# Wide products in a split-precision transformer kernel: one of 512 columns for two of 256

## The chip, the cores and the metric

The kernel runs on one core of a Trainium2 chip, in one launch. The metric is the device time of an execution in microseconds (us); the kernel before takes a median of 1346.6 us in three runs (1344.37 to 1347.13). A core has a matrix engine (PE, with its weight loads PEld), a vector engine (DVE), an activation engine (ACT), a general engine (POOL) and a queue engine (SP) that here issues nearly all DMAs. PE writes only into PSUM, which has 8 banks of 512 float32 columns; the other engines read the results from there.

## What is computed

The input has 256 tokens of width 1024. A first layer (adaLN modulation, grouped-query attention beside spatial gating, an output projection, then an expert-choice layer of 16 experts whose weights are streamed from HBM), a second layer of latent attention, and a third, "forgetting" layer are applied in turn. The two places that the change touches are these.

```
mix_l = jnp.concatenate([gqa_attend(ql, k_all, v_all),
                         spatial_gating(hl, w_gm, v_gain, w_s, b_s)], axis=-1)
xl_new = xl + gt1 * (mix_l @ w_out)              # first output projection, 256x1024 @ 1024x1024
xl_new = xl_new + gt2 * expert_choice_ffn(modulate(xl_new, g_ffn, sh2, sc2), ...)
```

The forgetting layer projects its normalised input to queries, keys, values, forget logits and gates (16 heads of 64). A running sum of the log forget gates along the tokens is added, as a difference between query and key positions, to the scores ahead of a causal softmax; the attended values are multiplied by a gate (a sigmoid, computed through tanh) and projected by `o_w_out`; a final norm follows.

## The kernel before

Every float32 operand of a large product is kept as two parts, hi (rounded by a cast on ACT) and lo (the rest, a subtraction on DVE or POOL), and a product is three: hi.hi, hi.lo and lo.hi, added up in PSUM (`mm3`, L142). With 256 tokens as columns each of the three is a product of 128x128 weights with 256 columns. `cols8(w, k, ...)` picks chunk k of 8 along the contracted width, from both parts.

The program is straight-line, and the order of the code is the order on each engine: nothing is rescheduled. PSUM tiles are given out by `bank`, which takes the first of a list of free banks, and `free` puts a bank back at the list's end; a matmul group that takes a bank waits until the engine that read it last is through. SBUF has 23 slots of 1 MB with the same kind of list, filled by DMAs on the SP queue when a slot comes free. `split` issues hi and lo of a weight tile. `later` collects DVE steps that `flush` puts out at fixed points.

First output projection (L948 on): 8 output tiles of 128 rows by 256 tokens, each 8 chunks of `mm3` and one DVE step that scales the product and adds it to the residual `xT`; squares for the norm and the router's logits follow tile by tile, and after the last the routing, the gather and the experts' first products `p_h`.

The forgetting layer: queries and keys are computed in tiles of 256 features (`q_tile`, `k_tile`: one bank for the two 128-feature chunks, transposed, features on partitions), evicted by `qk_scaled` (one DVE step for each chunk: product times scale times the row of reciprocal norms `rb2`). Values come in tiles of 256 features, tokens on partitions, evicted by ACT (`v_tile`). Gates come in 8 chunks (`gate`): a DVE step, tanh on ACT, a DVE step. The running sum of the log forget gates (`fx`) is a chain of small DVE and ACT steps, transposed as `p_ct`. Attention goes in 8 pairs of heads through a software pipeline: step i computes scores and softmax numerators of pair i (`soft_a`: `p_s` on PE, bias and row extremes on DVE, exponentials on ACT), transposes pair i-1 (`soft_b`), normalises pair i on DVE (`soft_n`) and multiplies pair i-2 with the values (`soft_c`, `p_o`). The table `fills` names the projections that go into each step in between, and `FSP` the splits of weights. For the first pair, q0, k0, v0, the norm row (`p_bc`), q1 and k1 go ahead.

## Time and profile before

| | |
|---|---|
| median of three runs | 1346.6 us |
| the profiled execution | 1347.84 us |
| its span in the profile | 1346.1 us |
| first output projection, in the trace | until 169.0 us |
| experts, mostly weight DMA | about 182 to 1060 us |
| forgetting layer's values, queries, keys, gates | 1214 to 1314 us |
| output projection and final norm | 1314 to 1346 us |

Times in the trace count from the span's start. Rows of a timeline give the start, the time the instruction took (its end may overlap the next one's start), the engine, the line, the operation, out<-in and the shapes. The rows used are shown in a section of their own, ahead of the prediction.

### The profile page before, as it was taken

Reading aid. Unit: us, or ns where it says so; the run is one execution under the profiler, and the core shown is the slowest. Engines: PE = TensorE matmul, PEld = TensorE weight load, DVE = VectorE, ACT = ScalarE, POOL = GpSimd, SP = SyncE. Lnnn points to the kernel's source line nnn. Section 1 sums busy time; section 2 is a strip of 40 time slices with the busy share of each in tenths; the row PEclk is TensorE's granted clock in tenths of the full one; section 3 lists DMA queues with packets and bytes.
Section 4 is the critical chain, followed back from the end, with each engine's and each line's share of the span. In section 5 each row is a group of like instructions: output and inputs, shape, how many; then the busy total and the mean of one; then the engine's idle time right before and its main releaser. Section 6 shows DMA issues by size and latency. Waiting matters only on the chain.

```text
span 1346.1 us, 16926 instructions
## 1 busy us (share of the span) xinstructions
PE 1072.6 (80%) x6795; PEld 516.1 (38%) x6795; DVE 436.1 (32%) x1172; ACT 266.5 (20%) x538; POOL 128.9 (10%) x181
## 2 busy tenths in 40 slices
PE   6999987777677687777767777776766799999998
PEld 3875942111112111111211111121111287899996
DVE  2756552111012011111201111120212168837974
ACT  2536410000000000000000000000000156653563
POOL 1000100000000000000000000000000113781530
PEclk9999999878978787887979888798888799999999
DMA  9997699999999999999999999999999993274230
GB/s 374 398 395 296 237 383 427 427 426 427 427 427 427 427 427 427 427 427 427 427 426 428 426 427 426 427 426 427 427 428 425 384 349 119 68 269 153 95 126 32
DMA packets 112638, 482.76 MB, mean 359 GB/s; under 512 B 8010, under 2 KB 57424, under 8 KB 61104
## 3 DMA queue, kind: packets, MB, share of 16 engines
q1 hardware_dynamic: 111456, 479.10, 87.0%
q0 software_dynamic: 848, 2.48, 0.6%
q8 instruction: 54, 0.88, 0.2%
q14 instruction: 24, 0.20, 0.0%
q10 hardware_dynamic: 256, 0.10, 0.0%
HBM read 480.59 MB, written 1.06 MB: 358 GB/s over the span
## 4 chain that ended last, share of the span: by engine, by line
DMA 63%; PE 29%; DVE 4%; POOL 2%; ACT 1%; issue 1%; ACTq 0%; SPq 0%; DVEq 0%; POOLq 0%
DMA w<-in_w_dram 63%; PE p_aT L136 5%; PE p_aN L136 3%; PE p_gate L136 3%; POOL lo L166 2%; PE p_out L136 2%; PE p_s L136 2%; PE p_oo L136 2%; PE p_y L136 1%; PE p_o L136 1%; PE p_h L136 1%; PE p_mod L136 1%; PE p_aF L136 1%; PE p_lat L136 1%; PE p_pt L1415 1%
## 5 line engine op out<-in xcount | busy, mean ns | idle before, releaser
L136 PE MATMUL p_y<-w,hidT 128*32 128x512 f32 (+1 forms) x1088 | 240.4, 631 | 65.7 <-DMA w<-in_w_dram 58.8
L136 PE MATMUL p_h<-w,rows_k 128*32 128x512 f32 x1024 | 169.2, 753 | 91.2 <-DMA w<-in_w_dram 91.1
L136 PE MATMUL p_h<-w,rows_q 128*32 128x512 f32 x1024 | 170.5, 759 | 82.4 <-DMA w<-in_w_dram 81.3
L166 POOL TENSOR_TENSOR lo<-w,hi 128x256 fp32r<-128x256 f32 (+1 forms) x136 | 102.4, 789 | 973.4 <-ACT hi L162 957.1
L136 PEld LDWEIGHTS p_y<-w,hidT 128*32 128x32 f32 x1088 | 56.0, 116 | 251.9 <-issue 144.5
L1152 DVE SCALAR_TENSOR_TENSOR ysl<-p_y,ig,ysh 128x512 fp32r<-128x512 f32 (+1 forms) x34 | 24.4, 719 | 267.5 <-ACT ysh L1151 266.0
L136 PEld LDWEIGHTS p_h<-w,rows_k 128*32 128x32 f32 x1024 | 24.2, 119 | 214.5 <-DMA w<-in_w_dram 189.4
L136 PEld LDWEIGHTS p_h<-w,rows_q 128*32 128x32 f32 x1024 | 24.9, 119 | 200.0 <-DMA w<-in_w_dram 171.0
L1151 ACT ACTIVATE ysh<-p_y,ig 128x512 fp32r<-128x512 f32 (+1 forms) x34 | 22.4, 662 | 398.2 <-PE p_y L136 398.2
L1053 DVE TENSOR_SCALAR oh<-p_ix,cst,rs 128x32 f32<-128x32 f32 x30 | 7.9, 306 | 267.5 <-PE p_ix L136 267.5
L1075 ACT COPY xr<-p_g 128x256 f32<-128x256 f32 x16 | 6.0, 372 | 420.2 <-PE p_g L136 420.2
L162 ACT CAST hi<-w 128x2048 fp32r<-128x2048 f32 (+3 forms) x41 | 71.3, 1759 | 26.4 <-DMA w<-in_e_w_in_dram 19.1
L166 DVE TENSOR_TENSOR lo<-w,hi 128x2048 fp32r<-128x2048 f32 (+2 forms) x24 | 48.2, 2026 | 24.0 <-ACT hi L162 22.8
L1156 DVE SCALAR_TENSOR_TENSOR xT<-p_sc,m,xT 128x256 f32<-128x256 f32 x128 | 51.8, 475 | 4.0 <-PE p_sc L136 4.0
L1138 DVE TENSOR_TENSOR hid<-s,p_h 128x512 f32<-128x512 f32 x16 | 11.0, 688 | 83.9 <-PE p_h L136 83.9
L136 PE MATMUL p_aT<-y2h,hi 128*128 128x256 f32 x128 | 36.8, 287 | 0.6 <-ACT y2h L1227 0.6
L136 PE MATMUL p_aT<-y2l,hi 128*128 128x256 f32 x128 | 36.3, 284 | 0.1
L136 PE MATMUL p_aT<-y2h,lo 128*128 128x256 f32 x128 | 36.2, 283 | 0.0
L1076 DVE COPY xr<-p_g 128x256 f32<-128x256 f32 x16 | 6.8, 425 | 84.1 <-ACT xr L1075 84.1
L1393 ACT ACTIVATE pr<-pr,st 128x128 f32<-128x128 f32 x64 | 28.5, 447 | 25.8 <-DVE st L1389 25.8
L1408 DVE TENSOR_SCALAR pr<-pr,st 128x128 f32<-128x128 f32 x64 | 30.9, 545 | 0.6
L136 PE MATMUL p_mod<-w,cm 128*32 128x512 f32 x192 | 26.7, 642 | 0.8 <-ACT cm L466 0.8
(491 smaller groups left out, 1709.7 us busy)
## 6 DMA issues: line engine op xcount, KB each, us to landing
w<-in_w_dram SPq DMA_DIRECT2D x376, 1024.0 KB, 19.6
w<-in_w_mod_dram SPq DMA_DIRECT2D x24, 1024.0 KB, 10.1
w<-in_o_w_in_dram SPq DMA_DIRECT2D x16, 1024.0 KB, 8.2
w<-in_w_dram SPq DMA_DIRECT2D x16, 512.0 KB, 8.0
w<-in_w_in_dram SPq DMA_DIRECT2D x7, 1024.0 KB, 17.3
...
```

The costliest lines, as they stand in the source:

```text
L136: PE.matmul(o, lhsT, rhs, start=start, stop=stop, skip_group_check=True)
L162: S.copy(r_(hi[:, c_]), t[:, c_])
L166: eng.tensor_tensor(r_(lo[:, d_]), t[:, d_], hi[:, d_], op=OP.subtract)
L1053: V.tensor_scalar(oh[b], p[:, 0:n], table(C_TCOL + b, 1), rs2[:, b:b + 1], op0=OP.is_equal, op1=OP.mult)
L1076: V.tensor_copy(t[:, 256:512], p[:, 256:512])
L1138: V.tensor_tensor(hid, s1, hp[1], op=OP.mult)
L1151: S.activation(r_(h), yp, AF.Copy, scale=g)
L1152: V.scalar_tensor_tensor(r_(l), yp, g, h, op0=OP.mult, op1=OP.subtract)
L1156: V.scalar_tensor_tensor(xT[:, m, :], p, gt2[:, m:m + 1], xT[:, m, :], op0=OP.mult, op1=OP.add)
L1393: S.activation(t[:, c0:c1], t[:, c0:c1], AF.Exp, bias=st[:, 2 * z + b:2 * z + b + 1], scale=-1.0, accum_out=st[:, 4 + 2 * z + b:5 + 2 * z ...
L1408: V.tensor_scalar(t[:, c0:c1], t[:, c0:c1], st[:, 8 + 2 * z + b:9 + 2 * z + b], None, op0=OP.mult)
L1415: PE.transpose(p[:, 128 * n:128 * n + 128], pt[:, 128 * n:128 * n + 128], ident)
```

## The change

The activation's hi and lo parts of one chunk are now stored side by side (`Sides`, `both`), 512 columns. `mm_wide` makes two products of the three: the hi weights with 512 columns (hi and lo of the activation at once), whose two halves of a bank are separate partial sums, and the lo weights with 256 columns, added to the right half. The two halves are added when the bank is evicted. In the first output projection this takes two dependent DVE steps for each tile. For queries and keys a tile takes two banks instead of one (`acc_W`), and each chunk's eviction is an ACT copy of the left half, a DVE addition of the right half and the DVE scaling, the last one now wholly in SBUF; gates likewise. Half of the values, v0 and v1, are turned round: the weight tiles are loaded as 512 input rows by 512 features (the same bytes), and the product has 512 features as its columns; `v_half(0)` runs where v0 stood, and `v_first` in pipeline step 2, in the place of v1, adds the second half and evicts both. Its two banks are held in between. v2 and v3, the second layer and everything else stay.

```diff
@@ -143,6 +143,28 @@
         mm(o, r_(l[0]), r_(r[0]), start, False)
         mm(o, r_(l[0]), r_(r[1]), False, False)
         mm(o, r_(l[1]), r_(r[0]), False, stop)
+
+    class Sides:
+
+        def __init__(self, ts, z):
+            self.ts, self.z = ts, z
+
+        def __getitem__(self, key):
+            _, k, c = key
+            a = 512 * (k % 4) + 256 * self.z
+            return self.ts[k // 4][:, a + (c.start or 0):a + (256 if c.stop is None else c.stop)]
+
+    def both(ts, k):
+        return ts[k // 4][:, 512 * (k % 4):512 * (k % 4) + 512]
+
+    def mm_wide(o, w, ts, k, start, stop):
+
+        y = both(ts, k)
+        if start:
+            mm(o, r_(w[0]), r_(y), True, False)
+        mm(o[:, 256:512], r_(w[1]), r_(y[:, 0:256]), False, False)
+        if not start:
+            mm(o, r_(w[0]), r_(y), False, stop)
 
     later = []
 
@@ -338,7 +360,12 @@
     ow_i = {part: {} for part in "qkvg"}
     for part, n in ("q0", "k0", "v0", "q1", "k1", "g0", "q2", "k2", "v1", "g1", "q3", "k3", "v2", "g2", "v3", "g3"):
         c0 = {"q": 0, "k": 1024, "v": 2048, "g": 3088}[part] + 256 * int(n)
-        ow_i[part][int(n)] = queue(cols(owi[:, c0:c0 + 256]))
+        if part == "v" and int(n) < 2:
+            r0 = 512 * int(n)
+            ow_i[part][int(n)] = queue((lambda t: t.rearrange("p (k n) -> p k n", k=4),
+                                        owi[r0:r0 + 512, 2048:2560].rearrange("(k p) n -> p k n", p=128)))
+        else:
+            ow_i[part][int(n)] = queue(cols(owi[:, c0:c0 + 256]))
     oo_i = [queue((lambda t: t.rearrange("p (k n) -> p k n", k=4),
                    o_w_out[0, 512 * a:512 * a + 512, 512 * n:512 * n + 512].rearrange("(k p) n -> p k n", p=128)))
             for n in range(2) for a in range(2)]
@@ -778,7 +805,8 @@
 
 
     mixh_, mixl_ = reuse(qr_, "mixh"), reuse(kr_, "mixl")
-    mixh, mixl = chunks(mixh_), chunks(mixl_)
+    mix = mixh_, mixl_
+    mixh, mixl = Sides(mix, 0), Sides(mix, 1)
     pr_ = [reuse(hh_, "pr0"), reuse(hl_, "pr1")]
     regions(pr_)
 
@@ -960,8 +988,10 @@
                 if m == 7 and n == 5:
                     sums(sq[6], False, False)
                     router(6)
-                mm3(p[:, 0:256], cols8(w, k, 128 * mi, 128 * mi + 128), (mixh[:, k, :], mixl[:, k, :]), n == 0, n == 7)
-            V.scalar_tensor_tensor(xT[:, m, :], p[:, 0:256], gt1[:, m:m + 1], xT[:, m, :], op0=OP.mult, op1=OP.add)
+                mm_wide(p, cols8(w, k, 128 * mi, 128 * mi + 128), mix, k, n == 0, n == 7)
+            for z in range(2):
+                V.scalar_tensor_tensor(xT[:, m, :], p[:, 256 * z:256 * z + 256], gt1[:, m:m + 1], xT[:, m, :],
+                                       op0=OP.mult, op1=OP.add)
             free(p)
             V.tensor_scalar(yT[:, m, :], xT[:, m, :], A2[:, m:m + 1], None, op0=OP.mult)
             if m:
@@ -1454,14 +1484,21 @@
             for g in f[2]:
                 g()
 
-    def gate(dst, w, mi, y, rb):
+    def gate(dst, w, mi, y, rb, ts=None):
 
         def f():
             p = bank("p_gate")
+            z, th = w2k("gz", 256), w2k("gth", 256)
             for k in range(8):
-                mm3(p[:, 0:256], cols8(w(), k, 128 * mi, 128 * mi + 128), y(k), k == 0, k == 7)
-            z, th = w2k("gz", 256), w2k("gth", 256)
-            V.scalar_tensor_tensor(z, p[:, 0:256], 0.5, rb, op0=OP.mult, op1=OP.mult)
+                w_ = cols8(w(), k, 128 * mi, 128 * mi + 128)
+                if ts:
+                    mm_wide(p, w_, ts, k, k == 0, k == 7)
+                else:
+                    mm3(p[:, 0:256], w_, y(k), k == 0, k == 7)
+            if ts:
+                S.copy(z, p[:, 0:256])
+                V.tensor_tensor(z, p[:, 256:512], z, op=OP.add)
+            V.scalar_tensor_tensor(z, z if ts else p[:, 0:256], 0.5, rb, op0=OP.mult, op1=OP.mult)
             free(p)
             S.activation(th, z, AF.Tanh)
             later.append(lambda: V.scalar_tensor_tensor(dst, th, 1.0, z, op0=OP.add, op1=OP.mult))
@@ -1725,7 +1762,8 @@
     free(gT_, qn_, kn_, mk["q"], mk["k"], *pr_)
 
     y2h_, y2l_ = slot("y2h"), slot("y2l")
-    y2h, y2l = chunks(y2h_), chunks(y2l_)
+    ys2 = y2h_, y2l_
+    y2h, y2l = Sides(ys2, 0), Sides(ys2, 1)
     y2 = lambda k, c0=0, c1=256: (y2h[:, k, c0:c1], y2l[:, k, c0:c1])
     fx_ = slot("fx")
     gf2 = fx_[:, 0:1024]
@@ -1733,6 +1771,15 @@
     nc.sync.dma_start(gf2, bass.AP(tensor=g_final_2.tensor, offset=g_final_2.offset, ap=[[0, 128], [1, 1024]]))
     p_st2 = bank("p_st2")
     A = []
+
+    def acc_W(w):
+
+        p = [bank("p_aW") for _ in range(2)]
+
+        def step(k):
+            for mi in range(2):
+                mm_wide(p[mi], cols8(w, k, 128 * mi, 128 * mi + 128), ys2, k, k == 0, k == 7)
+        return p, step
 
     def stats2(m):
         for b in range(2):
@@ -1761,7 +1808,7 @@
         if m2 == 1:
             W["v0"] = split(ow_i["v"][0])
         if m2 == 2:
-            A = [acc_T(W["q0"], y2), acc_T(W["k0"], y2)]
+            A = [acc_W(W["q0"]), acc_W(W["k0"])]
             for m in range(2):
                 first_steps(m)
         if m2 == 3:
@@ -1787,7 +1834,23 @@
         mm(p_f[32 * j:32 * j + 32, 0:256], wf[:, k, :], xT[:, k, :], k < 4, k > 3)
     W["q1"] = split(ow_i["q"][1])
     W["k1"] = split(ow_i["k"][1])
-    p_v0 = whole(acc_N(W["v0"], y2))
+    p_v = [bank("p_v") for _ in range(2)]
+
+    def v_half(n):
+
+        for k in range(4 * n, 4 * n + 4):
+            for b in range(2):
+                mm3(p_v[b], y2(k, 128 * b, 128 * b + 128),
+                    tuple(t[:, 512 * (k % 4):512 * (k % 4) + 512] for t in W["v%d" % n]), k == 0, k == 7)
+        freer("v%d" % n)()
+
+    def v_first():
+        v_half(1)
+        for b in range(2):
+            S.activation(v2[:, b, 0:512], p_v[b], AF.Copy, scale=r3[:, b:b + 1])
+        free(*p_v)
+
+    v_half(0)
     rb2 = bc_rows(r3, "rows_q")
 
     q2_, k2_, v2_ = slot("q2"), slot("k2"), slot("v2")
@@ -1796,9 +1859,11 @@
 
     def qk_scaled(dst, n, p, scl):
         for mi in range(2):
-            V.scalar_tensor_tensor(dst[:, 2 * n + mi, :], p[:, 256 * mi:256 * mi + 256], scl, rb2,
-                                   op0=OP.mult, op1=OP.mult)
-        free(p)
+            o = dst[:, 2 * n + mi, :]
+            S.copy(o, p[mi][:, 0:256])
+            V.tensor_tensor(o, p[mi][:, 256:512], o, op=OP.add)
+            V.scalar_tensor_tensor(o, o, scl, rb2, op0=OP.mult, op1=OP.mult)
+        free(*p)
 
 
     ct = fu
@@ -1838,19 +1903,19 @@
 
     def q_tile(n):
         def f():
-            qk_scaled(q2, n, whole(acc_T(W["q%d" % n], y2)), -0.125)
+            qk_scaled(q2, n, whole(acc_W(W["q%d" % n])), -0.125)
             freer("q%d" % n)()
         return f
 
     def k_tile(n):
         def f():
-            qk_scaled(k2t, n, whole(acc_T(W["k%d" % n], y2)), 1.0)
+            qk_scaled(k2t, n, whole(acc_W(W["k%d" % n])), 1.0)
             freer("k%d" % n)()
         return f
 
-    def v_tile(n, p=None):
+    def v_tile(n):
         def f():
-            p_ = p or whole(acc_N(W["v%d" % n], y2))
+            p_ = whole(acc_N(W["v%d" % n], y2))
             for b in range(2):
                 S.activation(v2[:, b, 256 * n:256 * n + 256], p_[:, 256 * b:256 * b + 256], AF.Copy,
                              scale=r3[:, b:b + 1])
@@ -1859,7 +1924,6 @@
         return f
 
     sp = lambda c, n, eng=None: splitter("%s%d" % (c, n), ow_i[c][n], 2048, eng)
-    v_tile(0, p_v0)()
     q_tile(1)()
     sp("g", 0)()
     sp("q", 2)()
@@ -1898,7 +1962,7 @@
                        lambda n, r0=r0, i=i: k2t[r0:r0 + 64, i, 0:n], fox_bias(h), None, 1.0))
             vs.append(lambda kb, h=h: v2[:, kb, 64 * h:64 * h + 64])
         pairs.append((qk, vs, fin(g2, o2h, o2l, i)))
-    g_ = [gate(g2[:, m, :], lambda m=m: W["g%d" % (m // 2)], m % 2, y2, rb2) for m in range(8)]
+    g_ = [gate(g2[:, m, :], lambda m=m: W["g%d" % (m // 2)], m % 2, y2, rb2, ys2) for m in range(8)]
     fr_g = [freer("g%d" % n) for n in range(4)]
     sp_o = [splitter("o%d" % n, oo_i[n], 2048) for n in range(4)]
     p_oo = {}
@@ -1922,7 +1986,7 @@
     fills = {
         0: ([g_[0]], [], [g_[1], fr_g[0]]),
         1: ([q_tile(2)], [o2_slots], [k_tile(2), spread_logs(1)]),
-        2: ([v_tile(1)], [], []),
+        2: ([v_first], [], []),
         3: ([g_[2]], [g_[3], fr_g[1]], []),
         4: ([q_tile(3)], [], []),
         5: ([k_tile(3)], [], []),
```

DVE between the scan of the log forget gates and the first pair's softmax (`bias` of `soft_a`). Before: `q` and `k` are the evictions of q1 and k1, `lo` the splits of g0, q2 and k2.

```order
L1826 SCALAR_TENSOR_TENSOR fx<-fx 16x256
L1799 SCALAR_TENSOR_TENSOR q_7041<-p_aT,rows_q 128x256 x2
L166 TENSOR_TENSOR lo<-w_6722,hi 128x2048
L166 TENSOR_TENSOR lo<-w_6724,hi 128x2048
L1799 SCALAR_TENSOR_TENSOR k_7042<-p_aT,rows_q 128x256 x2
L166 TENSOR_TENSOR lo<-w_6726,hi 128x2048
L1871 COPY ctc<-p_ct 128x32
L1878 SCALAR_TENSOR_TENSOR bias<-cs_7066,ctc,mask_123 128x128
```

After, in the same place:

```order
L1864 TENSOR_TENSOR q_6932<-p_aW,q_6932 128x256
L1865 SCALAR_TENSOR_TENSOR q_6932<-q_6932,rows_q 128x256
L1864 TENSOR_TENSOR q_6932<-p_aW,q_6932 128x256
L1865 SCALAR_TENSOR_TENSOR q_6932<-q_6932,rows_q 128x256
L188 TENSOR_TENSOR lo<-w_6666,hi 128x2048
L188 TENSOR_TENSOR lo<-w_6668,hi 128x2048
L1864 TENSOR_TENSOR k_6933<-p_aW,k_6933 128x256
L1865 SCALAR_TENSOR_TENSOR k_6933<-k_6933,rows_q 128x256
L1864 TENSOR_TENSOR k_6933<-p_aW,k_6933 128x256
L1865 SCALAR_TENSOR_TENSOR k_6933<-k_6933,rows_q 128x256
L188 TENSOR_TENSOR lo<-w_6670,hi 128x2048
L1935 COPY ctc<-p_ct 128x32
```

Four steps have become eight, and the three splits and the softmax stand behind them.

PE where pair 0's scores follow k1 and p_ct. Before:

```order
L136 MATMUL p_aT<-y2l,hi 128x256
L136 MATMUL p_aT<-y2h,lo 128x256
L1870 MATMUL p_ct<-ident,fx 128x16 x2
L136 MATMUL p_s<-k_7042,q_7041 128x128 x2
L136 MATMUL p_s<-k_7042,q_7041 128x256 x2
L136 MATMUL p_gate<-y2h,hi 128x256
L136 MATMUL p_gate<-y2l,hi 128x256
L136 MATMUL p_gate<-y2h,lo 128x256
```

After (`p_aW` is k1, `p_gate` gate 0):

```order
L136 MATMUL p_aW<-y2l,lo 128x256
L136 MATMUL p_aW<-y2l,hi 128x512
L1934 MATMUL p_ct<-ident,fx 128x16 x2
L136 MATMUL p_s<-k_6933,q_6932 128x128 x2
L136 MATMUL p_s<-k_6933,q_6932 128x256 x2
L136 MATMUL p_gate<-y2h,hi 128x512
L136 MATMUL p_gate<-y2h,lo 128x256 x2
L136 MATMUL p_gate<-y2h,hi 128x512
L136 MATMUL p_gate<-y2h,lo 128x256
```

The groups stand in the same order; the products in them are two for three.

ACT in pipeline steps 1 and 2, between the splits of weights and pair 2's exponentials (`pr`). Before:

```order
L162 CAST hi<-w_6785 128x2048
L1420 COPY PT<-p_pt 128x384
L162 CAST hi<-w_6787 128x2048
L1393 ACTIVATE pr_7191,st_7440<-pr_7191,st_7440 128x128
L1393 ACTIVATE pr_7191,st_7440<-pr_7191,st_7440 128x256
L1393 ACTIVATE pr_7191,st_7440<-pr_7191,st_7440 128x128
L1393 ACTIVATE pr_7191,st_7440<-pr_7191,st_7440 128x256
L1855 ACTIVATE v_7043<-p_aN,r_6942 128x256 x2
L1420 COPY PT<-p_pt 128x384
```

After:

```order
L184 CAST hi<-w_6729 128x2048
L1863 COPY q_6932<-p_aW 128x256 x2
L1450 COPY PT<-p_pt 128x384
L1863 COPY k_6933<-p_aW 128x256 x2
L184 CAST hi<-w_6731 128x2048
L1423 ACTIVATE pr_7066,st_7281<-pr_7066,st_7281 128x128
L1423 ACTIVATE pr_7066,st_7281<-pr_7066,st_7281 128x256
L1423 ACTIVATE pr_7066,st_7281<-pr_7066,st_7281 128x128
L1423 ACTIVATE pr_7066,st_7281<-pr_7066,st_7281 128x256
L1850 ACTIVATE v_6934<-p_v,r_6856 128x512 x2
L1450 COPY PT<-p_pt 128x384
```

The copies of q2 and k2 come in, and the values' eviction has 512 columns each and covers v0 and v1; it stands behind pair 2's exponentials, as v1's did.

## Rows read from the trace of the kernel before

**Rows 1.** The page, the chain that ended last, share of the span by engine.

```profile
DMA 63%; PE 29%; DVE 4%; POOL 2%; ACT 1%; issue 1%; ACTq 0%; SPq 0%; DVEq 0%; POOLq 0%
```

**Rows 2.** Busy us (instructions) by engine, clock, DMA share; four windows from 1220 summed.

```profile
1260.00:1280.00 20.00, 20.00 (x174) 17.83 (x171) 19.59 (x61) 14.36 (x36) 12.13 (x16) 1.00 0.18 54
...
sum 80.00, PE 80.00 PEld 74.57 DVE 69.49 ACT 43.84 POOL 30.51; mean PE 20.00 PEld 18.64 DVE 17.37 ACT 10.96 POOL 7.63
```

**Rows 3.** Waits of PE from 1195 us to the end: total, times, longest.

```profile
PE p_aT L136 <- ACT y2h L1227: 0.6, 1, 0.6
```

**Rows 4.** The chain, then PE's timeline: start us, us, what it was.

```profile
1203.47 8.64 PE p_aT L136 x72
...
1329.60 0.39 PE L136 MATMUL p_oo<-lo,o2h 128*128 128x512 f32 x1
...
1339.35 0.39 PE L136 MATMUL p_oo<-hi,o2l 128*128 128x512 f32 x1
```

**Rows 5.** First projection's end: DVE's timeline, the chain, a window.

```profile
169.03 0.48 DVE L964 SCALAR_TENSOR_TENSOR xT<-p_out,m,xT 128x256 f32<-128x256 f32 x1 [4.21 <-PE p_out L136]
...
181.59 7.07 PE p_h L136 x64
...
184.00:185.00 1.00, 1.00 (x12) 0.26 (x8) 0.93 (x4) 0.00 (x0) 0.00 (x0) 1.00 0.61 180
```

**Rows 6.** DVE's timeline in the last layer; in brackets idle before, releaser.

```profile
1220.60 0.42 DVE L1370 COPY rows_q<-p_bc 128x256 f32<-128x256 f32 x1 [0.84 <-PE p_bc L1368]
1221.06 0.76 DVE L1799 SCALAR_TENSOR_TENSOR q<-p_aT,rows_q 128x256 f32<-128x256 f32 x2
1221.74 0.75 DVE L1799 SCALAR_TENSOR_TENSOR k<-p_aT,rows_q 128x256 f32<-128x256 f32 x2
...
1223.27 0.41 DVE L1815 TENSOR_TENSOR fx<-fx 16x256 f32<-16x256 f32 x1
1223.72 0.41 DVE L1816 TENSOR_TENSOR fx<-fx,rows_q 16x256 f32<-16x256 f32 x1
...
1237.65 0.35 DVE L1878 SCALAR_TENSOR_TENSOR bias<-cs,ctc,mask 128x128 f32<-128x128 f32 x1
...
1240.08 0.42 DVE L1464 SCALAR_TENSOR_TENSOR gz<-p_gate,rows_q 128x256 f32<-128x256 f32 x1
...
1243.69 0.34 DVE L1878 SCALAR_TENSOR_TENSOR bias<-cs,ctc,mask 128x128 f32<-128x128 f32 x1
```

**Rows 7.** ACT's timeline, and ACT's group at line 1151 on the page.

```profile
1241.75 0.40 ACT L1466 ACTIVATE gth<-gz 128x256 f32<-128x256 f32 x1
...
1262.09 0.81 ACT L1855 ACTIVATE v<-p_aN,r 128x256 f32<-128x256 f32 x2
...
L1151 ACT ACTIVATE ysh<-p_y,ig 128x512 fp32r<-128x512 f32 (+1 forms) x34 | 22.4, 662 | 398.2 <-PE p_y L136 398.2
```

**Rows 8.** PE's timeline in the last layer, where a new group of products begins.

```profile
1220.12 0.38 PE L1368 MATMUL p_bc<-ident,r 128*128 128x128 f32 x2
...
1239.81 0.38 PE L136 MATMUL p_aT<-y2h,hi 128*128 128x256 f32 x1
...
1252.17 0.38 PE L136 MATMUL p_s<-k,q 64*128 64x128 f32 x2
...
1259.63 0.44 PE L136 MATMUL p_o<-PT,v 128*64 128x256 f32 x2
...
1285.19 0.38 PE L136 MATMUL p_s<-k,q 64*128 64x128 f32 x2
```

**Rows 9.** DVE's timeline, and the spread logs' tile: min/median/max ns.

```profile
1252.43 5.99 DVE L1408 TENSOR_SCALAR pr<-pr,st 128x128 f32<-128x128 f32 x4
...
1259.00 0.33 DVE L1878 SCALAR_TENSOR_TENSOR bias<-cs,ctc,mask 128x128 f32<-128x128 f32 x1
...
1284.49 0.75 DVE L1799 SCALAR_TENSOR_TENSOR k<-p_aT,rows_q 128x256 f32<-128x256 f32 x2
...
L1880 DVE SCALAR_TENSOR_TENSOR bias<-cs,ctc,mask x16: 472/478/960, 1237.9 to 1300.0; 128x256 f32<-128x256 f32 x16
```

## The prediction, made before the changed kernel ran

> **What bounds the kernel now.** I first read the page's chain of waits [rows 1]: 63% of it is DMA, in the expert stage above all, which this change doesn't touch. An average over the span says nothing here, so I went to the two stages that it does touch. In the last layer's stage, from 1220 to 1300 us, PE is busy 80.00 of 80.00 us [rows 2], and after 1195 us it waits once for another engine, for 0.6 us [rows 3]. PE sets the end there, so an instruction taken from PE should show one to one. The same windows show the second thing to see: DVE is busy 69.49 of those 80 us (19.59 of 20 from 1260 to 1280), so it has 10.51 us to spare, while ACT (43.84) has much. Whatever is moved from PE to DVE has to fit into these 10.51 us, and at the right places.
>
> **PE's saving.** A run of 72 products of 256 columns takes 8.64 us, 120.0 ns each; 43 products of 512 columns go from 1329.60 to 1339.35, 226.7 ns each [rows 4]. Two products of 256 in one of 512 so save 240.0 - 226.7 = 13.3 ns. Queries and keys have 8 tiles x 2 chunks x 8 = 128 such pairs, gates 64: 192 x 13.3 = 2.56 us. Two value tiles together have 16 steps of six products of 256 (720 ns), now three of 512 (680.1 ns): 16 x 39.9 ns = 0.64 us. The last layer saves 3.20 us, the first projection's 64 pairs 0.85 us, together 4.05 us. That the wide form gains nothing is out, since the kernel runs it already [rows 4]. The Trainium skill, page "TensorE: Matmul & The Clock Gate", section "Back-to-back issue gap", gives a lone warm product N/2.4 + 2.5 ns; by it a merged pair would save 2.5 ns and the 304 merges (256 pairs, 48 of the values) 0.76 us, an estimate. The trace, with 13.3 ns, differs, and the measurement decides.
>
> **First projection.** The last output tile's eviction lies on the chain (0.48 us at 169.03; DVE had waited 4.21 us for PE), and 12 us later come the first expert products [rows 5]. PE comes 0.85 us earlier; the last tile now has a second eviction step, dependent on the first: about 0.50 us (0.48, or the 0.45 us pitch of a dependent step, 1223.27 to 1223.72 [rows 6]). Net -0.35 us. It reaches the weight stream, since the DMA engines are only 0.61 busy from 184 to 185 us [rows 5], while these products still hold the slots that the next weights want. The other seven tiles' second steps lie in DVE's waits for PE. Ends: -0.85 (the step hidden) and +0.50 (the step paid, PE's gain lost to a late input). I take -0.35.
>
> **What the last layer pays on other engines.** Per chunk of 128x256, one step of DVE out of PSUM (two in 0.76 us, the next pair 0.68 us later, so 0.34 each [rows 6]) becomes an ACT copy, a DVE add and a dependent DVE step: 0.34 + 0.45 = 0.79 us, 0.45 more. 24 chunks: 10.8 us more for DVE (22 of them, 9.9 us, in the four windows with 10.51 us to spare), and 24 x 0.40 us (an ACT step of 128x256 [rows 7]) = 9.6 us for ACT. PE saves 3.2 us there and DVE pays over three times that.
> PSUM has 8 banks, taken from the front of a list and given back at its end. A q or k tile now takes two banks, and two more are held by the values from 1214 us until pipeline step 2. Following that list by hand through the order of the new code, q2 gets both banks of pair 0's scores and k2 both of pair 1's. So PE then waits for DVE's softmax there; in the kernel before, q2 and k2 each take one bank that is long free. Step by step:
> - PE comes to p_bc 0.74 us earlier (the first half of the values, q0 and k0). But q1 takes p_bc's bank, and so waits for the copy out of it, which before began 0.48 us after p_bc [rows 6, 8]: q1 starts at about 1220.35, as before, and the gain is spent.
> - Softmax of pair 0 begins on DVE at 1237.65 [rows 6]. Eight chunks (q0, k0, q1, k1) stand ahead: 8 x 0.45 = 3.6 us, less 0.6 for the earlier copy: +3.0.
> - q2 needs pair 0's banks, which DVE has read by about 1240.1 now [rows 6] and by 1243.1 then; before, q2 began at 1239.81 [rows 8]. PE stands about 3 us and ends q2 2.7 us late.
> - Gate 0's eviction waits for ACT's copy, which stands behind pair 0's exponentials. They end at 1241.75 now [rows 7], so at 1244.75, and pair 1's softmax begins 1.94 us after that end (1243.69 [rows 6]). Then: 1244.75 + 0.40 + 0.79 + 1.94 + 0.45 (gate 1's chunk) = 1248.3, and 2.43 us of softmax (as pair 0's, 1237.65 to 1240.08 [rows 6]) until its banks are free, 1250.8. k2's second chunk waits for that, and k2 ends at 1256.0 where pair 2's scores followed it at 1252.17 [rows 8]: +3.9.
> - The values' eviction is now one block for v0 and v1, on ACT behind pair 2's exponentials (at 1262.09 now [rows 7]), and p_o of pair 0, which needs only v0 and ran at 1259.63 [rows 8], must wait for it. Pair 2's softmax starts about 1.9 us later than 1259.00 and then lies beside POOL's subtractions, where a step of 0.48 us takes up to 0.96 [rows 9]: 1.1 us more, and the exponentials end at 1265.1, the first evicted half (0.66 us for 128x512 [rows 7]) at about 1265.75: p_o +6.1. Lower end: k2 late by 2.9 us only, and normalising pair 1 (5.99 us at 1252.43, beside POOL [rows 9]) no longer in the way: 1255.0 + 2.0 (k2's eviction, below) + 3.1 (softmax and exponentials, 1259.00 to 1262.09) + 0.66 = 1260.8, +1.1.
> - From there PE has slack ahead and gains on q3, k3, g2 and g3, and waits that it had are filled: -1.0.
> - Scores of pair 6 start at 1285.19 [rows 8], when k3's eviction (1284.49, 0.75 us [rows 9]) is just done. Two chunks then take 0.40 + 2 x 0.79 = 2.0 us instead of 0.68, behind pair 5's exponentials: +0.5 to +2.1; I take +1.0.
> - g4 to g7 save 32 x 13.3 ns = 0.4; the output projection behind them is PE's alone and follows rigidly.
> Sum: -0.35 + 6.1 - 1.0 + 1.0 - 0.4 = +5.35, ends -0.2 (-0.35 + 1.1 - 1.0 + 0.5 - 0.4) and +8.3 (+0.50 + 6.1 + 2.1 - 0.4, no catching up).
>
> **The rivals.** A, the other side: the saving comes through. Its place is q2 and k2: if DVE has read the scores' banks by the time PE comes, and the values by the time of p_o, nothing stands. The point is DVE's delay ahead of pair 0's softmax: below about 0.5 us, not the 3.0 worked out, as it would be if the new steps slipped into waits that I don't see. Then PE's saving is the whole effect and the time is 1347.84 - 3.20 - 0.35 = 1344.3, as a median 1343. For it: PE's 0.6 us of waits show a pipeline with grace [rows 3]. Against it: DVE's 16 of 20 us and the values' wait at p_o, which alone takes more than 1 us.
> B: the waits just eat the saving, the sum at its lower end, -0.2: 1347.6 profiled, 1346.4 as a median.
> C: the third step of each chunk reads two inputs from SBUF where before one came from PSUM. Steps of that kind (bias, 0.48 us) take 0.95 beside POOL's subtractions, and POOL is busy 30.51 of the 80 us [rows 2, 9]. If 9 of 24 meet it: 9 x 0.47 = 4.2 us more on a DVE that is by then the bound: about 1356. The Trainium skill, page "SBUF — State Buffer", section "Who interferes with whom", states it so: a DVE instruction with two SBUF inputs contends with a GpSimd one that reads SBUF, one with at most one such input doesn't. The rows of the bias agree, and it speaks against this change.
>
> **How the numbers follow.** The profiled run took 1347.84 us, 1.24 over the median 1346.6. 1347.84 + 5.35 = 1353.2; as a median 1352.0. Its own range is 1347 to 1355. Chances: forecast 0.52, A 0.17, B 0.15, C 0.16. The range holds the forecast, B and C, with 1 us for B's own spread and 2 for C's, and leaves A out: 1345.5 to 1358. About 0.2% (2.7 us) is what a measurement can tell from no change, 1343.9 to 1349.3: A is faster (0.17); B is the same (0.15), as is a little of the forecast (0.02); the rest of it and C are slower (0.66).
>
> **What would show it.** First, PE waiting for DVE at the starts of q2 and k2, some 3 and 1 us, and for ACT's eviction of the values ahead of p_o of pair 0; PE's busy time about 4 us less and the span longer all the same; DVE's busy time up by some 11 us, ACT's by 9 to 10. The first p_h at 181.2 rather than 181.59. If PE shows no waits from 1235 to 1266, the forecast is wrong and A holds; if p_o starts by 1261, B; if the steps that follow the adds have a mean above 0.6 us, C.

## The result, and the profile after

The changed kernel takes 1361.14 us at the median of three runs (1359.42 to 1366.23) against 1346.6: 1.011 times, with a 95% interval of 1.0084 to 1.0136. Run again later beside the kernel before, on another occasion, it gave 1.010 (1.0071 to 1.0128). It is slower, as forecast, but by 11 to 18 us where 5.4 were forecast, and outside the range of 1345.5 to 1358.

The profiled execution of the changed kernel took 1359.42 us, its span is 1357.3 us, 11.2 more than before. That pair of executions lies at the lower end of the interval; the medians are 14.5 us apart (13.5 on the later occasion), and no trace shows where the other 2 to 3 us lie. The page's line of engines:

```profile
PE 1078.6 (79%) x6491; PEld 502.1 (37%) x6491; DVE 447.6 (33%) x1204; ACT 273.4 (20%) x560; POOL 130.0 (10%) x181
```

DVE is busy 11.5 us more than before (436.1), ACT 6.9 more (266.5). PE has 304 products fewer. DVE's 32 additional steps are the 24 of the longer evictions and the 8 of the first output projection.

The answer to [rows 2], the last two of four windows of 20 us in the last layer and their sum: busy us (instructions) of PE, PEld, DVE, ACT, POOL, then the granted clock, the DMA share and GB/s.

```profile
1260.00:1280.00 20.00, 18.20 (x116) 14.37 (x115) 17.77 (x55) 12.30 (x32) 12.58 (x17) 1.00 0.35 109
1280.00:1300.00 20.00, 18.00 (x123) 15.06 (x122) 18.44 (x50) 10.04 (x26) 10.97 (x15) 0.91 0.32 106
sum 80.00, PE 72.69 PEld 58.74 DVE 69.07 ACT 42.77 POOL 26.34; mean PE 18.17 PEld 14.68 DVE 17.27 ACT 10.69 POOL 6.59
```

PE, busy 80.00 of 80.00 us before, now stands for 7.31 of them. DVE is as busy as it was (69.07 against 69.49), and its additional work has pushed the rest behind 1300 us. It isn't full in either trace: it stands idle for 10.9 us (10.5 before), as its steps wait for steps of ACT while others wait for it. What PE waits for from 1195 us to the end (us in total, times, longest) answers [rows 3]:

```profile
PE p_gate L136 <- DVE lo L188: 2.0, 2, 1.0
PE p_s L136 <- DVE k L1865: 2.0, 1, 2.0
PE p_aW L136 <- DVE st L1419: 1.8, 4, 0.6
PE p_o L136 <- ACT v L1850: 1.8, 1, 1.8
PE p_aW L136 <- DVE y2h L1258: 1.2, 1, 1.2
PE p_aW L136 <- DVE rows_q L1400: 0.7, 1, 0.7
```

9.5 us in ten waits, where there was one of 0.6: weight splits for gates 0 and 6, k3's eviction ahead of pair 6's scores, the scores' banks ahead of q2 and k2, the values' eviction, the lo part of y2, and the copy out of p_bc. The timelines of DVE, ACT and PE at the places of [rows 6] to [rows 9] (start us, us, what):

```profile
1240.84 0.35 DVE L1942 SCALAR_TENSOR_TENSOR bias<-cs,ctc,mask 128x128 f32<-128x128 f32 x1
...
1248.39 0.35 DVE L1942 SCALAR_TENSOR_TENSOR bias<-cs,ctc,mask 128x128 f32<-128x128 f32 x1
...
1260.66 0.82 DVE L1942 SCALAR_TENSOR_TENSOR bias<-cs,ctc,mask 128x128 f32<-128x128 f32 x1
...
1265.20 1.24 ACT L1850 ACTIVATE v<-p_v,r 128x512 f32<-128x512 f32 x2
...
1265.92 0.44 PE L136 MATMUL p_o<-PT,v 128*64 128x256 f32 x2 [1.79 <-ACT v L1850]
...
1293.20 1.46 PE L136 MATMUL p_s<-k,q 64*128 64x128 f32 x8 [2.00 <-DVE k L1865]
```

Softmax of pair 0 begins 3.2 us late (1237.65 before), that of pair 1 4.7 late (1243.69), that of pair 2 1.7 late (1259.00); the values are evicted at 1265.20; p_o of pair 0 is 6.3 us late and the scores of pair 6 8.0.

To compare kernels whose earlier stages differ by a few us from execution to execution, I use one stretch of each trace: from where PE begins to wait for the last layer's first product to the start of the last group of p_oo. It is 127.93 us before (1197.87 to 1325.80) and 138.55 changed (1197.81 to 1336.36): +10.62. All that lies ahead of it came out even in these two executions, to 0.06 us. How far the stretch repeats is shown by three kernels below whose last layer is the same: 138.55 us (changed), 138.52 (all) and 140.09 (no_first). So a difference of 1.5 us between two single traces shows nothing by itself.

### The profile page after: what moved, and what is told of

The parts are those of the page before. It is cut to its first block, busy times and chain, and to the rows that moved or that the text cites. A ratio compares the mean times of both kernels' runs of the same rounds, so it can differ in the third digit from the quotient of the medians.

```text
span 1357.3 us, 16383 instructions
## 1 busy us (share of the span) xinstructions
PE 1078.6 (79%) x6491; PEld 502.1 (37%) x6491; DVE 447.6 (33%) x1204; ACT 273.4 (20%) x560; POOL 130.0 (10%) x181
## 5 line engine op out<-in xcount | busy, mean ns | idle before, releaser
L136 PE MATMUL p_h<-w,rows_k 128*32 128x512 f32 x1024 | 175.3, 777 | 84.9 <-DMA w<-in_w_dram 84.9
L184 ACT CAST hi<-w 128x2048 fp32r<-128x2048 f32 (+3 forms) x41 | 71.5, 1761 | 26.8 <-DMA w<-in_e_w_in_dram 19.4
L1423 ACT ACTIVATE pr<-pr,st 128x128 f32<-128x128 f32 x64 | 28.5, 447 | 21.3 <-DVE st L1419 21.2
L1438 DVE TENSOR_SCALAR pr<-pr,st 128x128 f32<-128x128 f32 x64 | 26.8, 480 | 0.6
L136 PE MATMUL p_aW<-y2h,hi 128*128 128x512 f32 x64 | 23.9, 408 | 3.7 <-DVE st L1419 1.8
L136 PE MATMUL p_sc<-oh,ysh 128*128 128x256 f32 x128 | 22.5, 295 | 2.1 <-ACT ysh L1181 2.1
L136 PEld LDWEIGHTS p_sc<-oh,ysh 128*128 128x128 f32 x128 | 17.4, 189 | 15.7 <-ACT ysh L1181 15.7
## 6 DMA issues: line engine op xcount, KB each, us to landing
w<-in_e_w_out_dram SPq DMA_DIRECT2D x4, 1024.0 KB, 11.5
```

What stands on the lines that cost most here:

```text
L136: PE.matmul(o, lhsT, rhs, start=start, stop=stop, skip_group_check=True)
L184: S.copy(r_(hi[:, c_]), t[:, c_])
L1423: S.activation(t[:, c0:c1], t[:, c0:c1], AF.Exp, bias=st[:, 2 * z + b:2 * z + b + 1], scale=-1.0, accum_out=st[:, 4 + 2 * z + b:5 + 2 * z ...
L1438: V.tensor_scalar(t[:, c0:c1], t[:, c0:c1], st[:, 8 + 2 * z + b:9 + 2 * z + b], None, op0=OP.mult)
```

## The experiments

Theory E says that the longer evictions, on a DVE with little time to spare and behind ACT's exponentials, make PE wait. Theory B says that the doubled and held PSUM banks do, however short the evictions. Most kernels take each part of the change on or off by a set of names; a name that isn't in it takes the old code:

```diff
+WIDE = {"first", "v", "q0", "q1", "q2", "q3", "k0", "k1", "k2", "k3", "g0", "g1", "g2", "g3", "g4", "g5", "g6", "g7"}
...
+    def acc_qk(key):
+        return acc_W(W[key]) if key in WIDE else acc_T(W[key], y2)
```

| kernel | stretch, us | ratio to before (95%) |
|---|---|---|
| before | 127.93 | 1 |
| changed | 138.55 | 1.011 (1.0084 to 1.0136) |
| evict1 | 131.23 | 1.0024 (1.0011 to 1.0038) |
| no_values | 140.16 | 1.0082 (1.0052 to 1.0112) |
| no_k3 | 135.63 | 1.0055 (1.0034 to 1.0077) |
| no_gates | 135.48 | 1.005 (1.0034 to 1.0066) |
| evict3 | 140.84 | 1.0084 (1.0064 to 1.0104) |
| values | 132.11 | 1.0021 (1.0006 to 1.0035) |
| first | 127.90 | 0.9999 (0.9985 to 1.0014) |
| best | 130.22 | 1.0002 (0.999 to 1.0014) |
| act_copy | 128.74 | 1.0004 (0.9988 to 1.002) |
| dve_two | 139.30 | 1.0089 (1.0067 to 1.0111) |
| qk | 135.37 | 1.0069 (1.0048 to 1.0091) |
| best2 | 128.92 | 1.001 (0.9995 to 1.0024) |
| no_first | 140.09 | 1.0096 (1.0068 to 1.0124) |
| all (the change again) | 138.52 | 1.010 (1.0071 to 1.0128) |

The ratios compare medians of several executions, the stretch is of one trace each. The expectations of evict1, no_values, no_k3 and no_gates count from the first product to the end of p_oo, which is the stretch plus 13.95 us less the first wait (0.6 us before, 1.2 changed).

**evict1**, short evictions, banks and products as changed:

```diff
-            S.copy(o, p[mi][:, 0:256])
-            V.tensor_tensor(o, p[mi][:, 256:512], o, op=OP.add)
-            V.scalar_tensor_tensor(o, o, scl, rb2, op0=OP.mult, op1=OP.mult)
+            V.scalar_tensor_tensor(o, p[mi][:, 0:256], scl, rb2, op0=OP.mult, op1=OP.mult)
```

> The changed kernel with its products, banks and order as they are, but the evictions of queries, keys and gates reduced to one DVE step out of the left half (the right half's partial sums, hi.lo and lo.hi, are left out of the output). The last layer, from its first product of y2 to the end of p_oo, took 141.3 us before and 151.3 us changed. Theory E (the three-step evictions on a full DVE and behind ACT's exponentials make PE wait): the waits at q2, k2 and pair 6's scores go, PE's clock stays at 1.00 through v2, only the values' eviction ahead of pair 0's p_o is left (exponentials as before to 1262.1, plus 0.66, so +3.1, and PE saves 0.85 behind it): 143.5 us, total some 8 us below the changed kernel. Theory B (the doubled and held banks do it, however short the eviction): waits of 1 us and more at q2 and k2 stay, 147 us or more.

Measured: 144.0 us by that count (131.23 as the stretch), against 143.5 by theory E. PE's waits in this trace:

```profile
PE p_o L137 <- ACT v L1854: 3.1, 1, 3.1
PE p_aW L137 <- DVE y2h L1262: 1.2, 1, 1.2
PE p_aW L137 <- DVE rows_q L1404: 0.7, 1, 0.7
```

The waits at q2, k2, the splits and pair 6 are gone with the banks unchanged, and 7.3 of the 10.6 us with them. Theory B falls (act_copy, below, says the same). The expectation missed one thing: the clock was expected at 1.00 throughout, but fell behind the one wait that is left (shown below in the run values).

**no_values**, `"v"` taken out of the set:

> The changed kernel with v0 and v1 as before (narrow, one bank, own evictions), all else wide. Now q2 and k2 get banks of k1, of p_ct and of gates 0 and 1 instead of the scores'. Theory B (banks): no waits at q2 and k2, none ahead of pair 0's p_o; left are pair 6's scores (2.1 us), the lower clock behind them (1.5) and g6's wait for a split (1.0): last layer 146 us, some 5 to 6 us below the changed kernel. Theory E (evictions alone): only the wait ahead of p_o (1.8 us) goes, less 0.64 us of PE's saving: 150 us, 1 us below.

Measured: 152.9 us by that count, above either theory: with free banks for q2 and k2 the loss was not smaller. (It was 1.6 us larger in the stretch, about as much as no_first differs from the changed kernel.) PE's waits:

```profile
PE p_s L137 <- DVE k L1881: 3.6, 1, 3.6
PE p_gate L137 <- DVE lo L189: 2.4, 2, 1.4
PE p_aW L137 <- DVE y2h L1262: 1.2, 1, 1.2
PE p_aW L137 <- DVE st L1423: 0.9, 1, 0.9
PE p_aW L137 <- DVE q L1880: 0.7, 1, 0.7
PE p_aN L137 <- DVE q L1880: 0.5, 1, 0.5
PE p_aW L137 <- DVE rows_q L1404: 0.2, 1, 0.2
```

The waits at the scores' banks of pairs 0 and 1 and ahead of p_o did go, but other waits for DVE took their place, 3.6 us of them at pair 6's scores. This run doesn't weigh the banks alone, though: normalising pair 1 took 3.01 us of DVE where the changed kernel took 1.01, as POOL's split (first row) began ahead of it (what that does is shown below, at act_copy):

```profile
1255.85 6.13 POOL L189 TENSOR_TENSOR lo<-w,hi 128x256 fp32r<-128x256 f32 x8 [0.56 <-ACT hi L185]
...
1256.63 3.01 DVE L1442 TENSOR_SCALAR pr<-pr,st 128x128 f32<-128x128 f32 x4
```

**evict3**, the reverse: before's narrow products and banks, with three-step evictions (the lines are set against the kernel before; the dots stand for the rest of the call):

```diff
-            V.scalar_tensor_tensor(dst[:, 2 * n + mi, :], p[:, 256 * mi:256 * mi + 256], scl, rb2, ...)
+            S.copy(o, l)
+            V.tensor_tensor(o, l, o, op=OP.max)
+            V.scalar_tensor_tensor(o, o, scl, rb2, op0=OP.mult, op1=OP.mult)
```

> The kernel before with all its narrow products, its banks and its values, but queries, keys and gates evicted in three steps as in the changed kernel: an ACT copy, a DVE step of the product and the copy (a maximum of the two equal values in place of the addition), the DVE scaling in SBUF. From the end of PE's wait-free stretch ahead of y2's first product to the last group of p_oo PE took 127.9 us before, 138.6 us changed. Theory E (these evictions are the whole cost, and the wide products give PE's 2.6 us back where it waits anyway): 138 to 142 us, total 10 to 14 us above the kernel before. Theory B (doubled banks are needed for the harm): 128 to 130 us, at most 2 us above.

Measured: 140.84 us, +12.9, inside theory E's 138 to 142. Its largest waits are the changed kernel's, for k3's eviction and for splits:

```profile
PE p_s L137 <- DVE k L1877: 4.1, 1, 4.1
PE p_gate L137 <- DVE lo L189: 2.6, 2, 1.8
```

The evictions alone cost as much as the whole change. By the stretch they cost 2.3 us more, by the ratios (1.0084 against 1.010) not; whether the wide products give anything back isn't shown.

**act_copy and dve_two** ask which part of the eviction it is: ACT's copy in its place, or DVE's second step.

```diff
             S.copy(o, p[mi][:, 0:256])
-            V.tensor_tensor(o, p[mi][:, 256:512], o, op=OP.add)
             V.scalar_tensor_tensor(o, o, scl, rb2, op0=OP.mult, op1=OP.mult)
```

> The changed kernel with the addition left out of the evictions of queries, keys and gates: ACT copies the left half out of PSUM, DVE scales it in SBUF (the right half's sums are missing from the output). DVE has one step for each chunk as before the change, ACT its copy as in the changed kernel. Stretch to the last p_oo: 127.9 us before, 138.6 changed, 131.2 with the short eviction without a copy. Theory D (DVE's extra work makes PE wait): 131 to 133 us. Theory A (what counts is that the copies stand behind exponentials and casts in ACT's order): 135 to 138 us.

```diff
-            S.copy(o, p[mi][:, 0:256])
-            V.tensor_tensor(o, p[mi][:, 256:512], o, op=OP.add)
+            V.tensor_copy(o, p[mi][:, 0:256])
             V.scalar_tensor_tensor(o, o, scl, rb2, op0=OP.mult, op1=OP.mult)
```

> The changed kernel with DVE copying the left half out of PSUM and scaling it in SBUF, no ACT copy and no addition (the right half's sums are missing from the output): DVE has as many steps as in the changed kernel, ACT has none. Theory D: 135 to 139 us in the stretch that took 138.6. Theory A: 131 to 133 us.

Measured: 128.74 and 139.30 us. act_copy has the changed kernel's products, banks and ACT copies, and without DVE's addition nearly all of the loss is gone: it is DVE's second step (theory D). act_copy came out 2 us below theory D's range, and even below evict1, by timing: DVE's normalising of pair 1 and POOL's split of g1 collide in evict1 and don't in act_copy, where ACT's copies make that split begin later. The first two rows are of evict1's timelines of DVE and POOL, the next two of act_copy's:

```profile
1249.37 5.98 DVE L1442 TENSOR_SCALAR pr<-pr,st 128x128 f32<-128x128 f32 x4
...
1248.96 5.57 POOL L189 TENSOR_TENSOR lo<-w,hi 128x256 fp32r<-128x256 f32 x8
```

```profile
1258.09 1.01 DVE L1442 TENSOR_SCALAR pr<-pr,st 128x128 f32<-128x128 f32 x4
...
1260.02 6.16 POOL L189 TENSOR_TENSOR lo<-w,hi 128x256 fp32r<-128x256 f32 x8 [2.36 <-ACT hi L185]
```

The same four steps take 5.98 us or 1.01. The Trainium skill, page "SBUF — State Buffer", section "Who interferes with whom", lists tensor_scalar among the DVE operations whose two-port modes share a port pair with GpSimd; these rows fit that, though none shows the mode. (The prediction quotes that section for steps with at most one SBUF input without this exception.)

dve_two met the collision too, at another step. One scaling of q2, wholly in SBUF, took 5.54 us where the others took 0.42; the second row is POOL's:

```profile
1255.05 5.54 DVE L1879 SCALAR_TENSOR_TENSOR q<-q,rows_q 128x256 f32<-128x256 f32 x1
...
1254.74 5.57 POOL L189 TENSOR_TENSOR lo<-w,hi 128x256 fp32r<-128x256 f32 x8
```

PE then waited 4.82 us ahead of p_o, with a lower clock behind it. So runs are to be compared with runs alike in this. Without the collision, the changed kernel (its normalising took 1.01) against act_copy: 138.55 to 128.74, 9.8 us for the second step. With it, dve_two against evict1: 139.30 to 131.23, 8.1 us. What ACT's copies cost by themselves stays open, since the runs without them also have the collision. evict1 has it and the changed kernel doesn't, so that the 7.3 us between them are rather too few.

**no_k3**, `"k3"` alone taken out of the set:

> The changed kernel with tile k3 alone narrow again, in one bank and evicted by DVE alone. Theory 1 (pair 6's scores wait 2.0 us for k3's eviction behind pair 5's exponentials, and the granted clock falls because PE stood still): the wait goes, and v2 takes 5.9 us instead of 6.8 at a clock of 1.00 from 1290 to 1301; with 0.2 us lost on k3's products the last layer takes 151.3 - 2.0 - 1.5 + 0.2 = 148.0 us. Theory 2 (the clock falls there for another reason): the wait goes, the clock stays at 0.6 to 0.7 for some us, 149.5 us.

Measured: 148.4 us by that count, near theory 1's 148.0. A window of the changed kernel and one of this one, from pair 6's scores on:

```profile
1293.20:1296.00 2.80, 2.80 (x14) 2.15 (x15) 2.73 (x7) 1.38 (x2) 1.72 (x3) 0.54 0.01 3
```

```profile
1291.80:1294.60 2.80, 2.76 (x24) 2.43 (x25) 2.76 (x10) 2.56 (x3) 0.94 (x2) 1.00 0.30 116
```

With a wait of 0.5 us in place of 2.0 the clock stays at 1.00 and 24 products run where 14 did at 0.54. But theory 1's account of the gain is only half right, as the repeat of the changed kernel shows (**all**, below): there the clock did not fall behind the same wait, and the end came at the same place.

**no_gates**, all `"g"` names taken out:

> The changed kernel with the gates narrow again and evicted by DVE alone; queries, keys and v0, v1 wide. The banks go round as in the changed kernel. Theory E: q2's wait stays at about 1 us, since q0, k0, q1 and k1 still stand ahead of pair 0's softmax; k2's gets shorter by the copy behind the exponentials (0.4 + 0.45 us), g6's wait for its weights goes or halves, PE loses 0.85 us: last layer about 149.5 to 150.5 us. Theory B: unchanged waits, 152 us.

Measured: 148.2 us by that count, 1.3 below theory E's range: 8 of the 24 long evictions, and a third of the loss (3.1 of 10.6 us).

**qk**, queries and keys alone wide:

> The kernel before with queries and keys alone wide. Theory E: 16 of the 24 longer evictions, eight of them ahead of pair 0's softmax; q2 and k2 get banks that are free early, so PE waits at gate 0's split (1 to 1.5 us), and at pair 6's scores (1 to 3.6 us, with a lower clock behind them), against 1.7 us saved and 0.6 us lost where y2's first product now wants the lo part too: stretch 130 to 134 us against 127.9.

Measured: 135.37 us, above the range by 1.4. PE waits 2.9 us for k3's eviction and 1.4 for gate 0's split, and the clock was at 0.54 from 1290 to 1295, which the expectation names without a price.

**values**, v0 and v1 alone wide:

> The kernel before with v0 and v1 alone turned round and wide, in two held banks, evicted in pipeline step 2. Theory E (ACT's order: the eviction stands behind pair 2's exponentials, which end at 1262.1 as before): PE waits about 3.5 us ahead of pair 0's p_o, its clock falls behind that for about 0.7 us more, 0.64 us are saved: same stretch 131 to 132 us against 127.9. Theory S (the values' products save and the held banks are free in time): 127.3 us, a wait of under 0.5 us at p_o.

Measured: 132.11 us, +4.2, so theory E, with the one wait of 3.17 us at p_o. The timeline of PE there, then a window:

```profile
1258.90 1.55 PE L137 MATMUL p_o<-PT,v 128*64 128x256 f32 x8 [3.17 <-ACT v L1857]
1260.38 1.66 PE L137 MATMUL p_s<-k,q 64*128 64x128 f32 x8
...
1260.00:1262.00 2.00, 2.00 (x15) 1.02 (x11) 1.08 (x3) 1.89 (x2) 0.00 (x0) 0.50 0.03 9
```

At a clock of 0.50, the lower of the two levels (1.2 GHz), p_o takes 1.55 us where such a group takes 0.87 at 1.00, and the scores 1.66 where they take 0.93: 1.4 us more behind the wait.

**first**, the first projection alone wide:

> The kernel before with the first output projection alone wide. Theory F (64 pairs save 0.66 us as in the trace of the changed kernel, and the second eviction step costs 0.4 on the chain): from p_out's first product to p_y's first 57.8 us against 58.08 before, the last layer as before at 127.9, the total within 0.2%: 1344 to 1349 us. Theory C (the projection shortens PE's work enough that the granted clock falls in the routing behind it, as in the trace of the changed kernel): 61 us in that stretch and a total 3 us above.

Measured: the total is the same (0.9999), by theory F; the stretch from p_out to p_y, 61.30 us in its profile, is theory C's. It begins at 138.99 us here and at 141.72 before, so that its end differs by 0.5 us only. A window of the first expert products in this trace:

```profile
182.00:184.00 2.00, 2.00 (x12) 0.43 (x8) 1.86 (x8) 0.00 (x0) 0.00 (x0) 0.50 0.57 102
```

The clock is at its lower level there (1.00 in [rows 5]). In every trace, the kernel before included (172.85 to 176.26 us), it is at 0.50 once in the routing ahead; here it is so a second time. In the other traces that stretch from p_out to p_y took 57.8 to 58.1 us in five kernels with the wide projection and 59.4 to 61.2 in five, 57.9 to 58.1 in four with the narrow one and 59.5 in one. In the longer ones the lower clock in the routing lasts 6.8 us instead of 3.4, or comes a second time, as here: up to 3.2 us more. In the others the wide form gains at most 0.3.

**no_first and all**, the changed kernel without and with the first projection, on one chip:

> The changed kernel with the first output projection narrow as before, the whole last layer wide. Theory L (the last layer carries all of the loss): stretch 138.6 us, ratio to before 1.007 to 1.009, and the same as the changed kernel beside it within 0.2%. Theory C (the wide projection brings a lower clock in the routing and the first expert products, 3.2 us in that execution, and so the rest of the 14.5 us): 2 to 3 us below the changed kernel, p_out to p_y 57.9 to 58.1 us.

> The changed kernel again, for comparison with the run without the wide first projection on the same chip. Theory L: stretch 138.6 us, ratio 1.008 to 1.010. Theory C: ratio 1.010 to 1.012, and p_out to p_y 59.5 to 61.3 us where its first expert products run at half the clock.

Measured: 1360.18 and 1360.15 us at the median, no difference. Theory L holds: the last layer carries the loss. The stretch of no_first, 140.09, is 1.5 above its expectation, and the clock has it: behind its wait at p_o it fell, where it held at 1.00 in the changed kernel and in all.

```profile
1268.00:1271.00 3.00, 3.00 (x16) 2.17 (x13) 2.35 (x8) 3.00 (x7) 0.75 (x2) 0.52 0.51 181
```

From p_o to pair 5's scores it took 18.7 us, and all 17.1.

**best**, the first projection and the values, with the values' second half ahead of pair 2's scores:

```diff
-        1: ([q_tile(2)], [o2_slots], [k_tile(2), spread_logs(1)]),
-        2: ([v_first], [], []),
+        1: ([q_tile(2)], [o2_slots], [k_tile(2), spread_logs(1), v_first]),
+        2: ([], [], []),
```

> First output projection wide, and v0 and v1 wide with their second half and its eviction moved ahead of pair 2's scores, where ACT is idle; queries, keys and gates as before. Theory E: pair 2's scores have some 6 us of grace (DVE begins their softmax at 1259.0, PE has them ready at 1253.0), so nothing waits, the stretch to the last p_oo falls from 127.9 to 127.3 us, the total by 0.9 us to about 1346, inside what a measurement can tell. If the held banks cost anything, there is a wait of over 0.5 us at q2, k2 or p_o, and the stretch is 128 or more.

Measured: a ratio of 1.0002, but a stretch of 130.22 instead of 127.3. The wait at p_o is gone; gate 2, however, took 5.4 us instead of 3.0, because the split of its weights now stood behind the values' eviction on ACT and POOL began it at 1263.41.

**best2** puts that split ahead again, by adding the values' half behind it:

```diff
+    fills[1][2].append(v_first)
     pipeline(pairs, fills)
```

> As the run best, but with gate weights g1 split before the values' second half instead of after it: first output projection and v0, v1 wide, second half and eviction ahead of pair 2's scores; queries, keys and gates as before. Expected by theory E: no wait at p_o and none at gate 2, stretch 127.3 to 127.6 us against 127.9, total within 0.2% of before. If gate 2 or the scores still wait, 129 us or more.

Measured: 128.92 us, 1.001. Up to the scores of pair 5 it leads by 0.5 us, most of the values' saving of 0.64; at those of pair 6 PE waits 1.4 us for the narrow k3's eviction, which was just done in time before [rows 8, 9]. No version here beats the kernel before by more than a measurement can tell.

## Why the prediction was wrong

**The pace and the price of an eviction were right.** A longer eviction takes 0.46 us more of DVE at the mean, 0.45 were forecast, and 24 of them 11.1 us, against 10.8. That DVE's total rose by 11.5, as "some 11" had it, is luck: the total also holds 3.9 us of the first projection's second steps, which the 10.8 leave out, and other steps took 3.5 us less, normalising above all (30.9 to 26.8 us on the pages). ACT rose by 6.9, not 9 to 10. In evict1, where nothing waits there, k2 goes from 1243.67 to 1249.40, 5.73 us, 0.2 less than the 5.93 before, as 16 x 13.3 ns makes it.

**The places and the first sizes were right.** q1 waited for the copy out of p_bc (0.7 us), so the early gain was spent; half of it had already gone, as PE came to p_bc 0.4 us earlier and not 0.74 (y2's first product waited 1.2 us instead of 0.6, for the lo part too, which the sum leaves out). Softmax of pair 0: +3.0 forecast, +3.2 measured; pair 1's at 1248.3, measured 1248.39; q2's end +2.7, measured +3.1; k2's end 1256.0, measured 1256.43; the exponentials' end 1265.1, and the values' eviction began at 1265.20; p_o +6.1, measured +6.3. The +6.1 is in part luck: it rests on a start of pair 2's softmax "about 1.9 us later", for which the prediction gives no working, and the 1.7 measured came about by two large changes that cancel. The split on DVE ahead of q2's eviction began 4.5 us later (first row before, second changed), the evictions of q2 and k2 took 2.1 us more, and normalising pair 1 took 5 us less than the 5.99 of [rows 9], as only the lower end had it, since POOL's split began later:

```profile
1248.88 2.29 DVE L166 TENSOR_TENSOR lo<-w,hi 128x2048 fp32r<-128x2048 f32 x1 [2.16 <-ACT hi L162]
```

```profile
1253.40 2.29 DVE L188 TENSOR_TENSOR lo<-w,hi 128x2048 fp32r<-128x2048 f32 x1 [2.17 <-ACT hi L184]
...
1257.87 1.01 DVE L1438 TENSOR_SCALAR pr<-pr,st 128x128 f32<-128x128 f32 x4
```

Waits at q2 and k2 were smaller than written (1.0 and 0.8 us, not 3 and 1), as PE had already waited 1.0 us for gate 0's split and reached them later.

**What failed is everything behind p_o of pair 0**, three terms of the sum. By the stretch, counted as differences to before:

| place | forecast | measured |
|---|---|---|
| p_o of pair 0 | +6.1 | +6.35 |
| to pair 5's scores ("slack ahead and gains") | -1.0 | -0.15 |
| pair 6's scores, k3's eviction | +1.0 | +1.87 |
| to p_oo ("g4 to g7 save 0.4") | -0.4 | +2.55 |
| sum | +5.7 | +10.62 |

From p_o to pair 5's scores the forecast had PE gain, by its merged products and because "waits that it had are filled". But it had none to fill [rows 2, 3], and it has none there in the changed kernel:

```profile
1266.00:1290.00 24.00, 24.00 (x160) 19.27 (x161) 21.24 (x62) 14.04 (x34) 12.50 (x16) 1.00 0.26 84
```

The merged products of q3 and gates 2 and 3 gave 0.3 us, and p_o itself took 0.15 longer. What PE has lost by then it keeps: no_first lost another 1.5 us there to the clock and ended 1.5 us later. At pair 6's scores the mechanism was right, and the size was not: the wait for k3's eviction was 2.0 us, the upper end of what was written (+0.5 to +2.1), and +1.0 was taken.

The last term is the worst: it treated the stage from pair 6 on as PE's alone. In the changed kernel gate 6 waits for the split of its weights (the lo part, on DVE), and in **all** for the cast ahead of it on ACT and then for the same split. PE's timelines at gate 6, ACT's cast and DVE's split, first the changed kernel, then all:

```profile
1318.36 0.50 PE L136 MATMUL p_gate<-y2h,lo 128*128 128x256 f32 x2 [1.01 <-DVE lo L188]
...
1314.03 1.90 ACT L184 CAST hi<-w 128x2048 fp32r<-128x2048 f32 x1
...
1316.02 2.29 DVE L188 TENSOR_TENSOR lo<-w,hi 128x2048 fp32r<-128x2048 f32 x1 [1.17 <-issue]
```

```profile
1315.99 0.50 PE L137 MATMUL p_gate<-y2h,hi 128*128 128x512 f32 x1 [0.60 <-ACT hi L185]
...
1318.37 0.50 PE L137 MATMUL p_gate<-y2h,lo 128*128 128x256 f32 x2 [1.88 <-DVE lo L189]
...
1316.02 2.29 DVE L189 TENSOR_TENSOR lo<-w,hi 128x2048 fp32r<-128x2048 f32 x1 [1.17 <-issue]
```

In all the clock stayed at 1.00 behind pair 6's scores, PE was 1.5 us earlier at pair 7, and it waited that much longer: the split begins at 1316.02 in both. So the lower clock there cost nothing in the end. What sets the end is a chain of dependent steps on DVE and ACT, in their order: the softmax of pairs 6 and 7, the evictions of gates 4 and 5, then the cast on ACT and the split on DVE. From the start of pair 6's scores to the end of that split it takes 22.0 us before (1285.19 to 1307.22), just in time for gate 6 at 1307.44; 25.1 in the changed kernel and in all; and 22.3 in no_gates. DVE isn't full there either: it stood idle for 1.17 us ahead of the split, while ACT cast.

no_gates, which has no wait at gate 6, takes 40.6 us from pair 6's scores on (94.85 to 135.48 of the stretch), as the kernel before does (87.32 to 127.93), where the changed kernel takes 43.2. So the last term is the gates' evictions: the forecast gave their merged products a gain of 0.4, and left their eviction's place ahead of the next weights out.

In short, the step that failed is the path behind p_o of pair 0: there the forecast let PE set the pace, with -1.0 and -0.4, after it had counted DVE and ACT up to that point. The runs showed -0.15 and +2.55 in place of these, and +1.87 for the +1.0 between them.

**The first projection** was forecast at -0.35. Where the clock fell no more than before it is 0 to -0.3; in the profile it was +3.2, and that stage's early start (138.89 us, 141.72 before) hid that. It is nothing in the total (first, no_first). So that term missed in the profiled execution, and it didn't decide the result.

**The rivals.** A, the saving comes through, and B, the waits just eat it, didn't happen. C's mechanism is there and small in the changed kernel: the scaling in SBUF takes 425 ns at the median and at most 664, with means of 440 to 472 against the limit of 600 that was named; it isn't what was missing. It need not be small: in dve_two one such step took 5.54 us. That the changed kernel escaped this, and the collision that the kernel before has at normalising, is a matter of when POOL's split began. The forecast that PE's busy time falls by 4 us missed too: it rose by 6.0, 4.2 of them in the experts from 200 to 1060 us (p_h 344.2 us against 339.7; mean clock 0.84 against 0.85). The range ended at 1358 because C was taken as the worst case and the upper end of the sum, +8.3, left the last stage at -0.4.

**Open:** why the clock falls behind the same wait in one execution and not in the next; why the lower clock in the routing lasts longer or comes twice in six of eleven traces with the wide first projection and in one of five with the narrow one; and why the time from p_oo's last group to the span's end is 20.9 to 21.2 us in the traces of the changed kernel, of all and of no_first, where every other has 20.2 to 20.3. Up to DVE's last step it is 15.67 us in these three as in the kernel before, so the difference lies behind the last computation. None of it was tried by itself.
